# One transformer trunk layer on one core: the last down-projection group with its first transposes between the halves of its last product, embedding quarters around them, and the first two gate tiles in halves

## The chip, the cores and the metric

The kernel runs on one core of a Trainium2 chip. The metric is the device time of one execution in microseconds (us); lower is better. Times of a kernel are given as the median of several runs. A profile is of one execution; its span is the time from the first to the last instruction.

The engines are named as in the profile: PE is the tensor engine (matmuls; PEld is its weight loads), DVE the vector engine, ACT the scalar engine, POOL is GpSimd, and SP issues most DMAs.

## What is computed

The reference is one layer on 512 tokens of width 1024. A retention branch and a latent attention branch come first. Only the end of the layer matters here:

```
h2 = rms_norm(x, norm_mlp)
x = x + jnp.square(jax.nn.relu(h2 @ w_up)) @ w_down

gate = jax.nn.sigmoid(rms_norm(x, norm_ple) @ w_ple_gate)
x = x + gate * (p_l @ w_ple)
return x
```

`w_up` is 1024 x 4096, `w_down` 4096 x 1024, `w_ple_gate` 1024 x 1024, `p_l` 512 x 256 and `w_ple` 256 x 1024.

## The kernel before, in words

Every operand of a matmul is split into a high part and a low part (`split`, L289, and for weights `load_chunk`, L243: ACT writes the high part, L254, DVE the rest, L255), and each product is three matmuls: high by low, low by high, high by high (`mm3`, L279). A group of 24 matmuls of 512 columns makes one tile of 128 x 512 out of a 1024-long sum.

Weights come as blocks of 128 x 1024 (512 KB) through two helpers. `prepare` (L214) issues the DMA, up to three keys ahead; `load_chunk` splits the block, one key ahead. The split blocks have three buffers, the raw ones three or, for the down projection, seven. Some down blocks are sums of weight blocks: `prepare` has GpSimd issue a DMA that adds onto the raw block in SBUF (L225). Product 6's block is product 7's with one more block added, and product 4's is product 6's with another.

The work is a list of steps, (key of the weight, function, arguments), which is walked in order by `run_steps` (L258). Each engine gets its instructions from that list; a scheduler sets the order in which different engines' work interleaves within an engine, but PE keeps the list's order. So the order of steps around the change is the order on PE.

**The down projection** runs in four groups of 1024 rows of `w_down`. Each group is made by seven block products instead of eight, numbered 1 to 7: `combine` (L852) makes sums of activation blocks and splits them, `down` (L881) does one half (`c` = 0 or 1, 12 matmuls) of a product in PSUM, and `down_out` (L892) adds the product to `d`, the sum over groups. `d` is two tiles; its four blocks are c11, c12, c21, c22, and products go to them by the table in `down_out`: c11 is complete after products 1 and 2, c21 after 1, 6 and 4 (and what has been summed in PSUM), c22 after 5, and c12 after 3. Products 6, 5 and 3 accumulate in the PSUM tile of product 1, and 4 in that of 7 (`onto`, L879). In the first three groups the `up` products of the next group stand between these (`"u"` in `seq`, L1103). In the last group, which has none to prepare, `"u"` stands for a quarter of `p_l @ w_ple` (`ple`, L913, 12 matmuls and one ACT copy); in the trace its tile is `pw`.

**The end.** `reload_x2` (L923) reads x before the MLP back from DRAM into two tiles; `turn(n)` (L929, n = 0 to 3) transposes two column blocks of `d` by 8 instructions on PE (`tr`), adds them to x (L936), splits the result with the gain into `x3g` k = 2n and 2n + 1 (L937), and squares it for the norm (L941, summed in L945). `turn` 0 and 1 read c11 and c21; `turn` 2 and 3 read c12 and c22. `ple_gate(n)` (L952) multiplies eight tiles `x3g` by one tile of the gate's weight, into `pg`; `token_stats` (`stx`, L821) and `token_factor` (`pbx` on PE, copied to `bcx` by ACT, L829) make the norm's factor for each token; `ple_out` (L962) scales, applies the sigmoid, multiplies, adds and stores one tile of 128 rows of the output. The eighth tile is done in two halves of 256 tokens.

PSUM of this tail is a pool `PP` (L814) of four tiles, each of two banks.

Of the kernel before, what the change touches and what calls it, by code (L numbers as in the profile page):

```python
# [36 lines left out]
P = 128  # L37
# [17 lines left out]
GROUPS = DFF // 1024  # L55
# [89 lines left out]
def trunk_layer(ctx: ExitStack, tc: tile.TileContext, xT, pT, pos, gains, const, decay, wstream, outT):  # L145
# [18 lines left out]
    def MM(*a, **k):  # L164
        return tc.keep_in_program_order(nc.tensor.matmul(*a, **k))  # L165
# [38 lines left out]
    def step(key, fn, *args):  # L204
        steps.append((key, fn, args))
# [73 lines left out]
    def mm3(ps, stat, mov, first, last, **k):  # L279

        (sh, sl), (mh, ml) = stat, mov
        MM(ps, sl, mh, start=first, stop=False, **k)
        MM(ps, sh, ml, start=False, stop=False, **k)
        MM(ps, sh, mh, start=False, stop=last, **k)

    def cut(pair, a, n=P):
        return pair[0][:, a:a + n], pair[1][:, a:a + n]
# [30 lines left out]
    def stats(st, sq, rows=P, mov=None, first=True, last=True):  # L318

        mov = ones[0:rows, 0:1] if mov is None else mov  # L320
        for b in range(4):
            MM(st[:, b], sq[0:rows, b * P:b * P + P], mov, start=first and b == 0, stop=last and b == 3,
               skip_group_check=True)

    def blocks(ps, c):
        return ps[:, 0:4 * c].rearrange("p (b c) -> p b c", c=c)
# [8 lines left out]
    V = {}  # L335
# [54 lines left out]
    def mean_rsqrt(name, st, n):  # L390

        a, r = sm(name + "a"), sm(name, keep=True)
        TS(a, st.rearrange("p b c -> p (b c)"), 1.0 / n, EPS, op0=ALU.mult, op1=ALU.add)
        rsqrt(r, a, 4)
        return r, a
# [393 lines left out]
    x2g, x3g = [], [None] * 8  # L789
# [17 lines left out]
    def open_tail():  # L807
        head.close()
        t = tail.enter_context
        tail_pool["a"] = t(tc.tile_pool(name="tacts", bufs=1, reuse_waits="tile"))  # L810
        tail_pool["w"] = t(tc.tile_pool(name="tw", bufs=NDRAW, reuse_waits="tile"))
        tail_pool["p"] = t(tc.tile_pool(name="tpsum", bufs=4, space=bass.MemoryType.PSUM, reuse_waits="tile"))

    def PP(name):  # L814

        return tail_pool["p"].tile([P, 2, S], F32, tag="pp", name=name)
# [2 lines left out]
        return tail_pool["a"].tile([P, *shape], dtype, tag=tag, name=name, bufs=bufs)  # L819

    def token_stats(name, key):  # L821
        st = blocks(PP("st" + name)[:, 0], 1)
        stats(st, V[key])
        V["r" + name], _ = mean_rsqrt("r" + name, st, D)

# [123 lines left out]

    pg_ps = {}  # L950

    def ple_gate(w, n, cuts=1):  # L952
        N = S // cuts
        ps = PP(f"pg{n}")
        pg_ps[n] = []
        for c in range(cuts):
            out = ps[:, c, 0:N]
            for k in range(8):
                mm3(out, cut(w, k * P), cut(x3g[k], c * N, N), k == 0, k == 7)
            pg_ps[n].append(out)  # L960

    def ple_out(n):  # L962
        N = S // len(pg_ps[n])
# [52 lines left out]
    for h in range(MH):  # L1016
        p, more = h // 2, h + 2 < MH
# [69 lines left out]
    for n in range(8):  # L1087
        step(("o", n), out_proj, n)
    step(None, open_tail)

    def up_pair(gg, pair):
        for n in (2 * pair, 2 * pair + 1):
            step(("up", gg, n), up, gg, n)
            if (gg, n) == (0, 0):
                step(None, token_stats, "x2", "sq2")
            elif (gg, n) == (0, 1):
                step(None, token_factor, "x2")
        step(None, up_out, gg, pair)
# [4 lines left out]
    seq = [1, "u", 7, "u", 6, 2, "u", 5, 4, "u", 3]  # L1103
    order = [p for p in seq if p != "u"]
    step(None, combine, 0, 1)
    for gg in range(GROUPS):
        u = 0
        for p in seq if gg + 1 < GROUPS else [1, 7, "u", "u", 6, 2, 5, "u", 4, "u", 3]:
            if p == "u":
                if gg + 1 < GROUPS:  # L1110
                    up_pair(gg + 1, u)
                else:
                    if u == 0:
                        step(None, ple_in)
                    step(("ple", u // 2), ple, u)
                u += 1
                continue
            i = order.index(p)
            if p != 3:
                step(None, combine, gg, order[i + 1])  # L1120
            elif gg + 1 < GROUPS:
                step(None, combine, gg + 1, 1)
            if gg == GROUPS - 1 and p == 4:
                step(None, reload_x2)
            for c in range(2):
                step(("dp", gg, p, c), down, gg, p, c)
            step(None, down_out, gg, p)
    for n in range(4):
        step(None, turn, n)
    step(("pg", 0), ple_gate, 0)  # L1130
    step(None, token_stats, "x3", "sq3")
    step(("pg", 1), ple_gate, 1)
    step(None, token_factor, "x3")
    step(None, ple_out, 0)
    step(None, ple_out, 1)
    for n in range(2, 8):
        step(("pg", n), ple_gate, n, 2 if n == 7 else 1)
        step(None, ple_out, n)
    run_steps()

# [42 lines left out]
```

## Time and profile before

| | |
|---|---|
| median of 3 runs | 1153.18 us (1152.47 to 1153.44) |
| the profiled execution | 1154.78 us |
| its span, first to last instruction | 1153.0 us |
| mean granted PE clock | 0.998 of full speed |
| PE busy | 1125.0 us (98% of the span) |
| DVE busy | 699.9 us (61%) |
| ACT busy | 484.3 us (42%) |
| HBM traffic | 126.25 MB read, 4.19 MB written |

A row of the timeline has the start in us from the span's start, the duration, the engine, the source line, the operation and its operands as output<-inputs; instructions alike that follow each other are merged, with their count behind an x. In brackets stands how long the engine was idle before, and whose end released it. The chain of waits has start, duration and what ran. A row of the windows has the stretch, its length, busy time and count of PE, PEld, DVE, ACT and POOL, then the granted PE clock, the busy share of the DMA engines, and GB/s. PE's matmuls are pipelined: a row's duration overlaps the next row, so the pace is read from the starts.

### The profile page before, as it was taken

Reading aid. Unit: us, or ns where it says so; the run is one execution under the profiler, and the core shown is the slowest. Engines: PE = TensorE matmul, PEld = TensorE weight load, DVE = VectorE, ACT = ScalarE, POOL = GpSimd, SP = SyncE. Lnnn points to the kernel's source line nnn. Section 1 sums busy time; section 2 is a strip of 40 time slices with the busy share of each in tenths; the row PEclk is TensorE's granted clock in tenths of the full one; section 3 lists DMA queues with packets and bytes.
Section 4 is the critical chain, followed back from the end, with each engine's and each line's share of the span. In section 5 each row is a group of like instructions: output and inputs, shape, how many; then the busy total and the mean of one; then the engine's idle time right before and its main releaser. Section 6 shows DMA issues by size and latency. Waiting matters only on the chain.

```text
span 1153.0 us, 13664 instructions
## 1 busy us (share of the span) xinstructions
PE 1125.0 (98%) x5300; PEld 936.6 (81%) x5300; DVE 699.9 (61%) x1138; ACT 484.3 (42%) x682; POOL 29.1 (3%) x38
## 2 busy tenths in 40 slices
PE   7998999999999999999999999999999999999988
PEld 5877878888888888888888888788888888887766
DVE  5777586653447257545735766555466657667674
ACT  6446556442234243233324333434444434445531
POOL 0000000000000000000000000000001001001000
PEclk9999999999999999999999999999999999999999
DMA  6223131133212322321332234685567567567221
GB/s 202 69 71 108 47 87 47 55 124 107 92 55 92 121 74 69 107 92 55 110 103 73 74 97 147 185 300 138 137 188 173 150 180 170 162 173 175 92 73 55
DMA packets 43344, 133.42 MB, mean 116 GB/s; under 512 B 5296, under 2 KB 6576, under 8 KB 43024
## 3 DMA queue, kind: packets, MB, share of 16 engines
q1 hardware_dynamic: 38400, 115.36, 29.8%
q0 software_dynamic: 4736, 17.18, 8.5%
q8 instruction: 41, 0.67, 0.2%
q14 instruction: 23, 0.19, 0.0%
q10 hardware_dynamic: 144, 0.03, 0.0%
HBM read 126.25 MB, written 4.19 MB: 113 GB/s over the span
## 4 chain that ended last, share of the span: by engine, by line
PE 90%; DVE 5%; DMA 2%; ACT 1%; issue 1%; SPq 0%; DVEq 0%; ACTq 0%
PE up L165 15%; PE dn L165 11%; PE rg L165 8%; PE br L165 8%; PE rv L165 8%; PE rq L165 4%; PE rk L165 4%; PE gr L165 4%; PE bm L165 4%; PE pg L165 4%; PE gm L165 3%; PE ro L165 3%; PE wo L165 2%; PE sc L165 2%; PE pA L165 1%; PE pcq L165 1%
## 5 line engine op out<-in xcount | busy, mean ns | idle before, releaser
L254 ACT ACTIVATE wh_dp<-dr 128x1024 fp32r<-128x1024 f32 x56 | 59.2, 1061 | 121.0 <-PE up L165 83.6
L255 DVE TENSOR_TENSOR wl_dp<-dr,wh_dp 128x1024 fp32r<-128x1024 f32 x56 | 68.3, 1222 | 55.2 <-ACT wh_dp L254 55.2
L165 PE MATMUL dn<-wl_dp,ch 128*128 128x512 f32 x224 | 87.3, 390 | 0.7 <-DVE wl_dp L255 0.7
L165 PE MATMUL dn<-wh_dp,cl 128*128 128x512 f32 x224 | 87.2, 389 | 0.0
L165 PE MATMUL dn<-wh_dp,ch 128*128 128x512 f32 x224 | 87.2, 389 | 0.0
L254 ACT ACTIVATE wh_up<-wr_up 128x1024 fp32r<-128x1024 f32 x32 | 33.9, 1060 | 59.0 <-PE up L165 29.3
L225 POOL DMA_DIRECT2D dr<-wstream x32 | 27.6, 872 | 1029.0 <-DMA dr<-wstream 858.7
L165 PEld LDWEIGHTS dn<-wl_dp,ch 128*128 128x128 f32 x224 | 42.0, 188 | 9.9 <-DVE wl_dp L255 1.3
L255 DVE TENSOR_TENSOR wl_up<-wr_up,wh_up 128x1024 fp32r<-128x1024 f32 x32 | 39.1, 1223 | 17.7 <-ACT wh_up L254 17.6
L165 PEld LDWEIGHTS dn<-wh_dp,cl 128*128 128x128 f32 x224 | 42.0, 188 | 8.9
L165 PEld LDWEIGHTS dn<-wh_dp,ch 128*128 128x128 f32 x224 | 42.0, 188 | 8.6
L844 DVE SCALAR_TENSOR_TENSOR f<-up,bcx 128x512 f32<-128x512 f32 x32 | 20.6, 686 | 44.3 <-PE up L165 44.3
L255 DVE TENSOR_TENSOR wl_rg<-wr_rg,wh_rg 128x1024 fp32r<-128x1024 f32 x16 | 19.6, 1226 | 36.7 <-ACT wh_rg L254 36.7
L254 ACT ACTIVATE wh_rv<-wr_rv 128x1024 fp32r<-128x1024 f32 x16 | 17.0, 1060 | 55.3 <-PE br L165 26.2
L255 DVE TENSOR_TENSOR wl_rv<-wr_rv,wh_rv 128x1024 fp32r<-128x1024 f32 x16 | 19.6, 1226 | 32.8 <-ACT wh_rv L254 32.8
L254 ACT ACTIVATE wh_rg<-wr_rg 128x1024 fp32r<-128x1024 f32 x16 | 17.0, 1062 | 46.2 <-PE rv L165 35.0
L746 DVE TENSOR_TENSOR z<-rg,rbc 128x512 f32<-128x512 f32 x16 | 11.1, 692 | 39.7 <-PE rg L165 39.7
L254 ACT ACTIVATE wh_br<-wr_br 128x1024 fp32r<-128x1024 f32 x16 | 17.0, 1062 | 41.7 <-issue 18.8
L902 DVE TENSOR_TENSOR d<-d,dn 128x1024 f32<-128x1024 f32 x24 | 29.3, 1219 | 5.7 <-PE dn L165 5.7
L765 DVE TENSOR_TENSOR ret<-ret,br 128x512 f32<-128x512 f32 x24 | 16.5, 687 | 18.2 <-PE br L165 18.1
L622 ACT ACTIVATE p<-p,ng,hr 128x128 f32<-128x128 f32 (+3 forms) x32 | 20.7, 647 | 15.1 <-DVE ng L620 15.1
L255 DVE TENSOR_TENSOR wl_br<-wr_br,wh_br 128x1024 fp32r<-128x1024 f32 x16 | 19.5, 1220 | 3.5 <-ACT wh_br L254 3.5
(1590 smaller groups left out, 3383.5 us busy)
## 6 DMA issues: line engine op xcount, KB each, us to landing
dr<-wstream SPq DMA_DIRECT2D x40, 512.0 KB, 4.4
wr_up<-wstream SPq DMA_DIRECT2D x32, 512.0 KB, 4.3
dr<-wstream POOLq DMA_DIRECT2D x32, 512.0 KB, 5.8
wr_rv<-wstream SPq DMA_DIRECT2D x16, 512.0 KB, 3.4
wr_rg<-wstream SPq DMA_DIRECT2D x16, 512.0 KB, 3.5
wr_br<-wstream SPq DMA_DIRECT2D x16, 512.0 KB, 3.5
wr_gm<-wstream SPq DMA_DIRECT2D x16, 256.0 KB, 2.6
wr_bm<-wstream SPq DMA_DIRECT2D x8, 512.0 KB, 3.4
```

Of the source, the lines that this page charges most:

```text
L165: return tc.keep_in_program_order(nc.tensor.matmul(*a, **k))
L225: nc.gpsimd.dma_start(raw, chunk(("d", gg, kb, fb, c)), accum_op=ALU.add)
L254: ACT(hi, raw, AF.Copy)
L255: TT(lo, raw, hi.bitcast(F32), op=ALU.subtract)
L622: ACT(cols[b], cols[b], AF.Exp, bias=ng[:, b:b + 1], scale=d["rq"][:, b], accum_out=sums[:, b:b + 1])
L746: TT(z, ps, V["rbc"], op=ALU.mult)
L765: TT(ret[n], ret[n], ps, op=ALU.add)
L844: STT(u[:, i], ps[:, i], 0.0, V["bcx2"], op0=ALU.max, op1=ALU.mult)
L902: TT(to, to, dps[p], op=ALU.add if sign > 0 else ALU.subtract)
```

## The change

In the last group the order of products becomes 1, 7, 2, 6, 5, 4, 3. Two quarters of the embedding product stand after 2 and after 6; the other two move behind product 3. `turn(0)` and `turn(1)` stand between the two halves of product 3; `turn(2)` and `turn(3)` behind the last quarter. The reload of x2 is called at product 6 instead of 4. `ple_gate` can do half of the sum: tiles 0 and 1 first do k = 0 to 3 both, then k = 4 to 7 both. The third gate tile comes before the broadcast of the norm's factor, where the second did. The two halves of the eighth gate tile get a PSUM tile each. The PSUM tile for the statistics of x2 is taken when the tail's pools open.

```
     def ple_gate(w, n, part=None, cuts=1):
         N = S // cuts
         if n not in pg_ps:
             pg_ps[n] = [PP(f"pg{n}{c}")[:, 0, 0:N] for c in range(cuts)]
         for c, ps in enumerate(pg_ps[n]):
             for k in range(8) if part is None else range(4 * part, 4 * part + 4):
                 mm3(ps, cut(w, k * P), cut(x3g[k], c * N, N), k == 0, k == 7)
```

```
-        for p in seq if gg + 1 < GROUPS else [1, 7, "u", "u", 6, 2, 5, "u", 4, "u", 3]:
+        for p in seq if gg + 1 < GROUPS else [1, 7, 2, "u", 6, "u", 5, 4, 3]:
...
+            if gg == GROUPS - 1:
+                order = [1, 7, 2, 6, 5, 4, 3]
...
-            if gg == GROUPS - 1 and p == 4:
+            if gg == GROUPS - 1 and p == 6:
                 step(None, reload_x2)
             for c in range(2):
                 step(("dp", gg, p, c), down, gg, p, c)
+                if gg == GROUPS - 1 and p == 3 and c == 0:
+                    step(None, turn, 0)
+                    step(None, turn, 1)
             step(None, down_out, gg, p)
-    for n in range(4):
-        step(None, turn, n)
-    step(("pg", 0), ple_gate, 0)
+    step(("ple", 1), ple, 2)
+    step(("ple", 1), ple, 3)
+    step(None, turn, 2)
+    step(None, turn, 3)
+    for part in range(2):
+        for n in range(2):
+            step(("pg", n), ple_gate, n, part)
     step(None, token_stats, "x3", "sq3")
-    step(("pg", 1), ple_gate, 1)
+    step(("pg", 2), ple_gate, 2)
     step(None, token_factor, "x3")
     step(None, ple_out, 0)
     step(None, ple_out, 1)
-    for n in range(2, 8):
-        step(("pg", n), ple_gate, n, 2 if n == 7 else 1)
+    step(None, ple_out, 2)
+    for n in range(3, 8):
+        step(("pg", n), ple_gate, n, None, 2 if n == 7 else 1)
         step(None, ple_out, n)
```

What it moves on the engines is shown at three places, with the numbers that the built program gives its tiles. The first is PE at the border between the two halves of product 3 of the last group (`dn31` is the PSUM tile of products 1, 6, 5 and 3; `dp_3_3_0` and `dp_3_3_1` are the two halves' weights). Before:

```order
L165 MATMUL dn31_8316<-wh_dp_3_3_0_8604,cl33_8579 128x512
L165 MATMUL dn31_8316<-wl_dp_3_3_0_8605,ch33_8578 128x512
L165 MATMUL dn31_8316<-wh_dp_3_3_0_8604,ch33_8578 128x512
L165 MATMUL dn31_8316<-wh_dp_3_3_1_8637,cl33_8579 128x512
L165 MATMUL dn31_8316<-wl_dp_3_3_1_8638,ch33_8578 128x512
L165 MATMUL dn31_8316<-wh_dp_3_3_1_8637,ch33_8578 128x512
```

After:

```order
L165 MATMUL dn31_8316<-wl_dp_3_3_0_8584,ch33_8561 128x512
L165 MATMUL dn31_8316<-wh_dp_3_3_0_8583,ch33_8561 128x512
L165 MATMUL tr0_8620<-cst_80,d0_6682 128x128 x2
L165 MATMUL tr0_8620<-cst_80,d1_6683 128x128 x2
L165 MATMUL tr0_8620<-cst_80,d0_6682 128x128 x2
L165 MATMUL tr0_8620<-cst_80,d1_6683 128x128 x2
L165 MATMUL tr1_8640<-cst_80,d0_6682 128x128 x2
L165 MATMUL tr1_8640<-cst_80,d1_6683 128x128 x2
L165 MATMUL tr1_8640<-cst_80,d0_6682 128x128 x2
L165 MATMUL tr1_8640<-cst_80,d1_6683 128x128 x2
L165 MATMUL dn31_8316<-wh_dp_3_3_1_8602,cl33_8562 128x512
L165 MATMUL dn31_8316<-wl_dp_3_3_1_8603,ch33_8561 128x512
```

Sixteen transposes, those of column blocks 0 to 3, moved in front of the second half.

The second is DVE from product 4's addition to `d` on (`d1` += `dn37`; `dn31` is then product 3's, `x30` and `x31` are the reloaded x, `wl_pg` the low part of a gate tile's weight, `wl_ple` that of the embedding's). Before:

```order
L902 TENSOR_TENSOR d1_6683<-d1_6683,dn37_8358 128x2x512
L255 TENSOR_TENSOR wl_dp_3_3_1_8638<-dr_33111_8590,wh_dp_3_3_1_8637 128x1024
L255 TENSOR_TENSOR wl_pg_0_8656<-wr_pg_0_8608,wh_pg_0_8655 128x1024
L255 TENSOR_TENSOR wl_pg_1_8760<-wr_pg_1_8641,wh_pg_1_8759 128x1024
L902 TENSOR_TENSOR d0_6682<-d0_6682,dn31_8316 128x2x512
L936 TENSOR_TENSOR x30_8582<-x30_8582,tr0_8674 128x1024
L936 TENSOR_TENSOR x30_8582<-x30_8582,tr1_8694 128x1024
L298 SCALAR_TENSOR_TENSOR x3g0l_8685<-x30_8582,gn_81,x3g0h_8684 128x512
L936 TENSOR_TENSOR x31_8584<-x31_8584,tr2_8715 128x1024
L298 SCALAR_TENSOR_TENSOR x3g1l_8689<-x30_8582,gn_81,x3g1h_8688 128x512
```

After:

```order
L903 TENSOR_TENSOR d1_6683<-d1_6683,dn37_8358 128x2x512
L255 TENSOR_TENSOR wl_ple_1_8662<-wr_ple_1_8587,wh_ple_1_8661 128x1024
L937 TENSOR_TENSOR x30_8465<-x30_8465,tr0_8620 128x1024
L937 TENSOR_TENSOR x30_8465<-x30_8465,tr1_8640 128x1024
L298 SCALAR_TENSOR_TENSOR x3g0l_8631<-x30_8465,gn_81,x3g0h_8630 128x512
L255 TENSOR_TENSOR wl_pg_0_8681<-wr_pg_0_8606,wh_pg_0_8680 128x1024
L298 SCALAR_TENSOR_TENSOR x3g1l_8635<-x30_8465,gn_81,x3g1h_8634 128x512
L946 TENSOR_TENSOR sq30_8638<-sq30_8638,sq31_8658 128x1024
L298 SCALAR_TENSOR_TENSOR x3g2l_8651<-x30_8465,gn_81,x3g2h_8650 128x512
L903 TENSOR_TENSOR d0_6682<-d0_6682,dn31_8316 128x2x512
L298 SCALAR_TENSOR_TENSOR x3g3l_8655<-x30_8465,gn_81,x3g3h_8654 128x512
L255 TENSOR_TENSOR wl_pg_1_8760<-wr_pg_1_8665,wh_pg_1_8759 128x1024
```

The additions of the first two transposes and their four splits moved ahead of the addition of product 3, and the two gate weights' splits moved among them. Behind these rows follow `x31` += `tr2`, `x31` += `tr3`, and the rest up to `x3g7l`, with the split of gate tile 2's weight among them.

The third is PE at the broadcast of the norm's factor (`pbx3`), with what each row waits for in brackets. Before:

```order
L165 MATMUL pg1_8816<-x3g7h_8750,wh_pg_1_8759 128x512
L165 MATMUL pbx3_8841<-cst_80,rx3_8796 128x128 [waits DVE_49,PE_49]
L165 MATMUL pbx3_8841<-cst_80,rx3_8796 128x128 x3
L165 MATMUL pg2_8866<-x3g0h_8684,wl_pg_2_8811 128x512 [waits PE_49]
L165 MATMUL pg2_8866<-x3g0l_8685,wh_pg_2_8810 128x512
```

After:

```order
L165 MATMUL pg20_8847<-x3g7h_8750,wh_pg_2_8778 128x512
L165 MATMUL pbx3_8872<-cst_80,rx3_8827 128x128 [waits DVE_49,PE_49]
L165 MATMUL pbx3_8872<-cst_80,rx3_8827 128x128 x3
L165 MATMUL pg30_8903<-x3g0h_8630,wl_pg_3_8842 128x512 [waits Activation_49]
L165 MATMUL pg30_8903<-x3g0l_8631,wh_pg_3_8841 128x512
```

The tile behind the broadcast is now the fourth gate tile, and its first matmul waits for ACT; in the built program that is ACT's copy of the broadcast, and `pbx3` and `pg30` lie in the same two PSUM banks (`pbx3` and `pg2` did not).

More of the change, by code (lines that the diff above doesn't have):

```diff
@@ L812, in open_tail @@
         tail_pool["p"] = t(tc.tile_pool(name="tpsum", bufs=4, space=bass.MemoryType.PSUM, reuse_waits="tile"))
+        V["stx2"] = PP("stx2")
     def PP(name):
@@ L821, in token_stats @@
     def token_stats(name, key):
-        st = blocks(PP("st" + name)[:, 0], 1)
+        st = blocks((V["stx2"] if name == "x2" else PP("st" + name))[:, 0], 1)
         stats(st, V[key])
@@ L950, in trunk_layer @@
     pg_ps = {}
-    def ple_gate(w, n, cuts=1):
+    def ple_gate(w, n, part=None, cuts=1):
         N = S // cuts
[L954 to L960, printed above, removed]
+        if n not in pg_ps:
+            pg_ps[n] = [PP(f"pg{n}{c}")[:, 0, 0:N] for c in range(cuts)]
+        for c, ps in enumerate(pg_ps[n]):
+            for k in range(8) if part is None else range(4 * part, 4 * part + 4):
+                mm3(ps, cut(w, k * P), cut(x3g[k], c * N, N), k == 0, k == 7)
     def ple_out(n):
```

## The prediction

> **What bounds the kernel now.** I read the page first, then the chain that ended last over the final 93 us, then the tensor engine's (PE's) timeline where that chain leaves it, then the clock by windows. The page's first line says where the time is:
>
> ```profile
> PE 1125.0 (98%) x5300; PEld 936.6 (81%) x5300; DVE 699.9 (61%) x1138; ACT 484.3 (42%) x682; POOL 29.1 (3%) x38
> ```
>
> PE has work nearly all the time, so an edit that leaves its work alone can only win what PE waits, or loses to a slower clock. The chain of waits, with columns start, duration and what ran, shows where that is:
>
> ```profile
> 1061.75 10.95 PE dn L165 x47
> 1072.69 2.72 PE pw L165 x12
> 1075.41 5.44 PE dn L165 x24
> ...
> 1090.19 2.35 DVE x L936 x2
> 1092.54 0.66 DVE x3g0l L298
> 1093.20 1.13 DVE x L936
> ...
> 1098.59 1.14 DVE sq L945
> ...
> 1106.82 7.19 PE pg L165 x24
> 1114.01 0.44 PE pbx L165 x4
> 1114.44 32.99 PE pg L165 x168
> ```
>
> Up to 1089 and after 1106 the chain lies on PE; between them it lies on the vector engine (DVE), which turns the last sum `d` into the gate product's input. A matmul of the 512-wide kind costs 5.44/24 = 0.227 us in the row at 1075.41; the 24 at 1106.82 take 7.19. PE's timeline has the waits themselves (in brackets: idle before, and who ended it):
>
> ```profile
> 1049.67 0.39 PE L165 MATMUL pw<-pph,wl_ple 128*128 128x512 f32 x1
> ...
> 1061.75 0.50 PE L165 MATMUL dn<-wl_dp,ch 128*128 128x512 f32 x1 [0.70 <-DVE wl_dp L255]
> ...
> 1072.53 0.39 PE L165 MATMUL pw<-pph,wl_ple 128*128 128x512 f32 x1
> ...
> 1088.86 3.65 PE L165 MATMUL tr<-cst,d 128*128 128x128 f32 x32
> 1092.27 0.48 PE L165 MATMUL pg<-x3g0h,wl_pg 128*128 128x512 f32 x1
> 1093.26 0.50 PE L165 MATMUL pg<-x3g0l,wh_pg 128*128 128x512 f32 x1 [0.51 <-DVE x3g0l L298]
> ...
> 1105.87 0.94 PE L165 MATMUL stx<-ones,sq 128*128 128x1 f32 x8
> 1106.68 0.64 PE L165 MATMUL pg<-x3g0h,wl_pg 128*128 128x512 f32 x1
> ```
>
> **What is there to win.** Three losses, each a stretch of PE less its work.
> (a) From the first embedding matmul `pw` at 1049.67 to the next pair's at 1072.53 are 22.86 us, for 24 `pw` and 72 `dn`, 96 x 0.2267 = 21.76. Lost 1.10, most of it at 1061.75, where DVE's split of a weight block came late.
> (b) From the first transpose at 1088.86 to 1106.68 are 17.82 us, for 32 transposes (3.41 to the first `pg`), 24 matmuls (5.44) and the sums `stx` (0.81). Lost 8.16.
> (c) The next 24 matmuls take 7.17 us (1106.68 to the broadcast `pbx` at 1113.85, quoted below) instead of 5.44. Lost 1.73, to the clock: the column behind the engines' is the granted clock,
>
> ```profile
> 1080.00:1100.00 20.00, 16.65 (x85) 12.79 (x83) 16.24 (x17) 12.14 (x15) 0.00 (x0) 1.00 0.16 54
> 1106.00:1108.00 2.00, 2.00 (x13) 1.71 (x12) 0.98 (x7) 1.06 (x1) 0.00 (x0) 0.71 0.00 0
> 1108.00:1110.00 2.00, 2.00 (x6) 1.61 (x5) 1.86 (x7) 0.00 (x0) 0.00 (x0) 0.50 0.00 0
> ```
>
> half speed just after a dozen microseconds in which PE mostly waited. Together 10.99 us.
>
> **Part by part.** *Product order and embedding quarters.* PE's rows are the same as before to the end of product 7, at 1049.67 (the first `pw` row). Without waits PE then runs, at 2.72 us per half product or quarter: product 2 to 1055.11, quarter 0 to 1057.83, 6 to 1063.27, quarter 1 to 1065.99, 5 to 1071.43, 4 to 1076.87, first half of 3 to 1079.59, 16 transposes to 1081.29, second half to 1084.01, quarters 2 and 3 to 1089.45, 16 transposes to 1091.15. The question is whether everything arrives. Products 6 and 4 read a weight block onto which GpSimd's DMA adds; the issues, and ACT's first use of what they left:
>
> ```profile
> 1044.37 0.86 POOL L225 DMA_DIRECT2D dr<-wstream  x1 [0.83 <-DVE wl_dp L255]
> 1054.49 0.86 POOL L225 DMA_DIRECT2D dr<-wstream  x1 [9.26 <-DVE wl_dp L255]
> ...
> 1055.66 1.06 ACT L254 ACTIVATE wh_dp<-dr 128x1024 fp32r<-128x1024 f32 x1 [2.71 <-DMA dr<-wstream]
> ...
> DMA to landing us min/median/max: 3.4/5.4/11.2
> ```
>
> Product 6's second half landed at 1055.66, 11.2 us after its issue. It is now wanted at 1060.55 instead of 1057.83; with 1.06 on ACT and 1.22 on DVE (a 1024-wide instruction, worked out below) behind the landing, it has 2.5 us of room. The queue that the moved steps pass is SP's, where these stood:
>
> ```profile
> 1047.51 0.33 SPq L240 DMA_DIRECT2D wr_pg<-wstream  x1
> 1061.72 0.33 SPq L221 DMA_DIRECT2D dr<-wstream  x1
> ...
> 1070.06 0.43 SPq L926 DMA_DIRECT2D x<-x2d  x1
> ...
> x<-x2d SPq DMA_DIRECT2D x1, 1024.0 KB, 5.8
> ```
>
> The last block of product 3 (1061.72) now goes out when product 2's block is split, about 1047, in the place of the gate tile's load of equal size; that load and the 1 MB reload of half of x2 follow about 1052.5. So the traffic that meets product 6's block is the same till its last 3 us. Product 4's additions are issued as before (about 1055 and 1058) and wanted, with the 2.3 us of their splits, at 1069 and 1072; 11.2 us still make it. GpSimd's own order is unchanged. The other splits, 1.06 and 1.22 each and one per 2.72 us of matmuls, come out 1 us or more ahead of their halves. I take nothing for a wait here, with 2 us as the bound, and the whole of (a) as won.
>
> *First transposes between the halves.* They need column blocks c11 and c21 of `d`, whose last addition follows product 4: 1076.87, 0.2 till a matmul's end is seen (a row of 0.39 us stands in a slot of 0.23), and 1.22 (two such in the row at 1090.19 take 2.35, of which the chain counts 1.13 till the next begins): 1078.3, before PE is through the first half at 1079.59. 2.72 us of matmuls cover it; without them it would cost 1.4.
> Then DVE is the question. From the first addition of x (`tr0` ends at 1080.44, DVE starts 0.2 later) to `x3g7l`, the last input of the gate product, it has by its order eleven 1024-wide instructions and eight 512-wide ones: at the chain's 1.14 and 0.66, and 0.1 for the last one's end, 17.9, plus 0.4 in which it waits for the third transposes: done at 1098.95. PE, not waiting, has 12 + 12 gate matmuls with k below 4 (to 1096.59) and reaches `x3g7l` at 1098.86, ten matmuls into the next part. **The two chains meet within 0.2 us.** What hid nothing before now hides nearly all: 2.72 + 5.44 + 5.44 us of product 3, quarters and gate tile 1 stand beside DVE's work. I charge 0.17 of waiting; ahead is PE's bound, so this can only fall to 0, and each microsecond that DVE is late costs one. Of (b) and (c), then, all but 0.17 is won: PE is never half idle for long, so I take the clock to stay at 1.00.
>
> *The new wait.* In the new program the broadcast `pbx` and gate tile 3 have the same pair of PSUM banks, as three tiles now live at once; tile 3 must wait till ACT has copied the broadcast. Before, the same copy stood behind a weight split on ACT and nobody waited for it:
>
> ```profile
> 1113.85 0.60 PE L165 MATMUL pbx<-cst,rx 128*128 128x128 f32 x4
> 1114.05 1.06 ACT L254 ACTIVATE wh_pg<-wr_pg 128x1024 fp32r<-128x1024 f32 x1 [6.92 <-PE pg L165]
> 1114.20 0.48 PE L165 MATMUL pg<-x3g0h,wl_pg 128*128 128x512 f32 x1
> 1115.01 0.58 ACT L829 ACTIVATE bcx<-pbx 128x512 f32<-128x512 f32 x1
> ```
>
> The split waits for the last matmul ahead of the broadcast and is now tile 5's, with the same relation. So PE, which went on at 1114.20, goes on at 1115.59: 1.39 us lost. Queued behind are gate tiles 3 to 7, so all of it shows. Nothing would be lost if the slots differed; I see no way to more than 1.6.
>
> *The last tile.* Its halves were two slices of one PSUM tile, now two tiles:
>
> ```profile
> 1147.46 0.76 DVE L967 TENSOR_TENSOR zg<-pg,bcx 128x256 f32<-128x256 f32 x2 [2.94 <-PE pg L165]
> 1147.92 0.75 ACT L968 ACTIVATE zg<-zg 128x256 f32<-128x256 f32 x2 [4.85 <-DVE zg L967]
> 1148.37 0.76 DVE L969 TENSOR_TENSOR zg<-zg,pw 128x256 f32<-128x256 f32 x2 [0.15 <-ACT zg L968]
> 1149.05 0.75 DVE L970 TENSOR_TENSOR zg<-zg,x 128x256 f32<-128x256 f32 x2
> 1149.49 0.81 SPq L971 DMA_DIRECT2D outT<-zg  x2
> ```
>
> The first half waited for the second. Now it can leave during the second's 2.7 us of matmuls, and one half runs after PE: multiply at 1147.46, sigmoid 1147.92, multiply 1148.37, add 1148.83 (one 0.42 later), store 1149.27, where the second store left at about 1149.92. 0.65 won; between 0 and 0.8.
>
> *The PSUM tile of the x2 statistics* is taken earlier; its slot and that of the first `up` tile stay the same: nothing.
>
> **The sum.** 10.99 + 0.65 - 0.17 - 1.39 = 10.08. The span of 1153.0 becomes 1142.9, the profiled execution's 1154.78 becomes 1144.7; the runs' median of 1153.18, 1.6 below that execution, becomes **1143.1 us**.
>
> [...] The row: 32 transposes in a run, 1088.86 to 1092.27, lie in the window 1080 to 1100, whose granted clock is 1.00. [...]
>
> **Rivals.** *DVE late.* The two chains are so close that a delay anywhere among 19 instructions shows, with waits `[.. <-DVE x3g..]` at k 4 to 7 and, if long, a piece of (c). At 0.5 to 3 us, typically 1.5: 1144.6. For: in that stretch DVE waits in turn for ACT's high parts and PE's transposes, and the row at 1093.26 shows PE waiting for just these outputs. Chance 0.20.
> *Weights late.* Product 6's block lands 1 to 3 us after its room, as the 1 MB reload shares the DMA engines: 1145.1. Against: 2.5 us of room. 0.07.
> *Clock.* A half-speed stretch like that of (c) appears behind the transposes: 1.73 each, for two 3.46: 1146.6. 0.05.
> *No overlap.* The first transposes release nothing, say since the reload of x2 comes late; then (b) and (c) come back and only (a) and the last tile are won, less the new wait: 1152.8. Against: the reload is issued some 27 us before its use. 0.03.
> *Slower.* Product 4's added block, issued behind the reload, is so late that PE stands. It costs from a landing at 1069 on, one for one; beyond the kernel before by over 0.2% (2.3 us) it needs 10.1 + 2.3 = 12.4 us, a landing at 1081.4, 26 us after the issue, where the longest row above is 11.2: 1155.5. 0.02.
>
> **How the numbers follow.** The forecast has 0.63. Its own range is 1141.7 (no new wait) to 1144. With DVE late and weights late it reaches to 1146.2, and 1141.5 below takes in the bound of the last tile: that holds over 8 in 10, the clock's single stretch included. About 0.2%, 2.3 us, can be told from no change here: faster 0.95 (all but the last two), same 0.03, slower 0.02.
>
> **What would show it.** Right: PE without a gap over 0.3 us from 1050 to the first `pg` matmul at about 1091; `stx` near 1102; a gap of 1.4 ended by ACT `bcx` ahead of tile 3 (near 1109); clock 1.00 in every window from 1080; one half chain behind PE. Wrong: a `dn` matmul that waits for `wl_dp`, gaps ended by `x3g` with k above 3, clock below 1.00, or a tile 3 that doesn't wait.

## The result and the profile after

The changed kernel takes 1145.17 us (median of 4 runs, 1144.17 to 1146.36); the kernel before took 1153.31 beside it (4 runs, 1152.47 to 1155.58). The ratio is 0.9927, with a 95% interval of 0.9910 to 0.9944: 8.1 us faster, where 10.1 were forecast (1143.1). The profiled execution took 1144.94 us with a span of 1143.2; the forecast for it was 1144.7 and 1142.9. In the runs further below, one of e5's ten executions, the profiled one, took 2298.57 us; it is left out of e5's median and ratio, and e11 is the profile of that kernel.

PE's row on the page shows that the work stayed and the waiting went: 5300 matmuls as before, busy time 4.9 us less (1125.0 before), in a span that is 9.8 us shorter.

```profile
PE 1120.1 (98%) x5300; PEld 935.0 (82%) x5300; DVE 700.0 (61%) x1138; ACT 484.9 (42%) x682; POOL 29.1 (3%) x38
```

The chain of waits of the changed kernel, over the stretch that the prediction worked through:

```profile
1065.99 13.60 PE dn L165 x60
1079.59 1.75 PE tr L165 x16
1081.34 2.75 PE dn L165 x12
1084.09 5.44 PE pw L165 x24
1089.53 1.75 PE tr L165 x16
1091.28 11.14 PE pg L165 x48
1102.42 0.79 PE stx L165 x8
1103.21 5.62 PE pg L165 x24
...
1108.85 1.06 ACT wh_pg L254
1109.91 0.49 ACT bcx L830
...
1110.44 27.86 PE pg L165 x144
...
1138.33 0.44 DVE zg L967
...
1138.79 0.42 ACT zg L968
...
1139.23 0.43 DVE zg L969
...
1139.69 0.42 DVE zg L970
```

Where the chain of before left PE for 16 us (1089.0 to 1105.3), nearly all of them on DVE, this one stays on PE from 1066 to 1109. It leaves PE for the copy of the broadcast, which stands behind a weight split on ACT, and again for one half tile at the end. The last 24 matmuls ahead of the broadcast take 5.62 where they took 7.19. The windows (columns as before, the granted clock behind the engines') show full speed, and PE without a pause until the new wait:

```profile
1080.00:1090.00 10.00, 10.00 (x55) 8.52 (x54) 9.50 (x10) 7.44 (x10) 0.00 (x0) 1.00 0.31 107
1090.00:1100.00 10.00, 10.00 (x51) 8.20 (x50) 9.10 (x11) 6.40 (x9) 0.00 (x0) 1.00 0.30 105
1100.00:1105.00 5.00, 5.00 (x27) 4.26 (x26) 2.81 (x8) 1.84 (x2) 0.00 (x0) 1.00 0.30 104
1105.00:1110.00 5.00, 4.25 (x21) 3.30 (x19) 1.49 (x8) 1.15 (x2) 0.00 (x0) 1.00 0.32 106
```

PE's timeline has one row with a wait from 1085 to the end:

```profile
1110.44 0.50 PE L165 MATMUL pg<-x3g0h,wl_pg 128*128 128x512 f32 x1 [1.19 <-ACT bcx L830]
```

DVE's timeline shows why PE no longer waits for it. Its chain now starts at 1080.50 and is through at 1098.89, beside product 3, the quarters and half the gate tiles; the addition of product 3 to `d` stands in the middle:

```profile
1080.50 2.35 DVE L937 TENSOR_TENSOR x<-x,tr 128x1024 f32<-128x1024 f32 x2 [1.24 <-PE tr L165]
...
1087.03 1.22 DVE L903 TENSOR_TENSOR d<-d,dn 128x1024 f32<-128x1024 f32 x1
...
1090.44 2.35 DVE L937 TENSOR_TENSOR x<-x,tr 128x1024 f32<-128x1024 f32 x2 [0.40 <-PE tr L165]
...
1098.15 0.74 DVE L298 SCALAR_TENSOR_TENSOR x3g7l<-x,gn,x3g7h 128x512 fp32r<-128x512 f32 x1
```

### The profile page after: what moved, and what is told of

It is laid out like the page before. It is cut to its first block, busy times and chain, and to the rows that moved or that the text cites. A ratio compares the mean times of both kernels' runs of the same rounds, so it can differ in the third digit from the quotient of the medians.

```text
span 1143.2 us, 13662 instructions
## 1 busy us (share of the span) xinstructions
PE 1120.1 (98%) x5300; PEld 935.0 (82%) x5300; DVE 700.0 (61%) x1138; ACT 484.9 (42%) x682; POOL 29.1 (3%) x38
## 3 DMA queue, kind: packets, MB, share of 16 engines
HBM read 126.25 MB, written 4.19 MB: 114 GB/s over the span
## 4 chain that ended last, share of the span: by engine, by line
PE 93%; DVE 3%; DMA 2%; ACT 1%; issue 0%; SPq 0%; ACTq 0%; DVEq 0%
PE up L165 15%; PE dn L165 13%; PE rg L165 8%; PE br L165 8%; PE rv L165 8%; PE pg L165 4%; PE rq L165 4%; PE rk L165 4%; PE gr L165 4%; PE bm L165 4%; PE gm L165 3%; PE ro L165 3%; PE wo L165 2%; PE sc L165 2%; PE pcq L165 1%; PE rs L165 1%
## 5 line engine op out<-in xcount | busy, mean ns | idle before, releaser
L254 ACT ACTIVATE wh_rv<-wr_rv 128x1024 fp32r<-128x1024 f32 x16 | 17.0, 1060 | 55.3 <-PE br L165 26.2
```

What stands on the lines that cost most here:

```text
L254: ACT(hi, raw, AF.Copy)
```

## Experiments

The theory was the prediction's sum. The gain is PE's waits for DVE (b), together with a late weight block (a) and the half clock (c), less a new wait of 1.4 us. The first rival was that one part does the work alone: the new order, the halves of the gate tiles or the last tile. The second was that the place of the transposes decides, by far more than the tie of 0.17. A third question came up with the first runs: why the medians moved by 8 to 9 us when the two profiles differ by 10.

Executions of one kernel reach the first `up` matmul at different times (747.5 to 750.6 in the 13 profiles here), long before the change. So the profiles are compared by the time from that matmul to the end of the span, called the *stretch*. For before it is 1153.0 - 748.9 = 404.1 us, and for after 1143.2 - 748.75 = 394.4. A median has those up to 3.1 us in it, so a difference of a microsecond or two between medians of six runs is read with care.

| kernel | median us (runs) | ratio to before [95%] | span - first `up` = stretch |
|---|---|---|---|
| e1 after, unchanged | 1144.47 (6) | 0.9923 [0.9908, 0.9938] | 1144.1 - 749.7 = 394.4 |
| e2 turns behind product 3 | 1146.81 (6) | 0.9936 [0.9921, 0.9952] | 1145.3 - 750.5 = 394.8 |
| e3 gate tiles whole | 1148.72 (6) | 0.9956 [0.9939, 0.9972] | 1146.8 - 749.7 = 397.1 |
| e4 broadcast in its own banks | 1143.51 (6) | 0.9916 [0.9899, 0.9933] | 1141.3 - 748.4 = 392.9 |
| e5 quarters and order as before | 1151.58 (9) | 0.9984 [0.9972, 0.9995] | (e11) |
| e6 before + new order | 1153.07 (10) | 0.9990 [0.9976, 1.0005] | 1151.5 - 747.7 = 403.8 |
| e7 before + gate halves | 1151.54 (10) | 0.9982 [0.9970, 0.9994] | 1150.6 - 750.4 = 400.2 |
| e8 before + last tile | 1153.23 (10) | 1.0002 [0.9990, 1.0014] | 1151.7 - 749.9 = 401.8 |
| e9 before, one run | 1153.14 (1) | | 1151.3 - 750.0 = 401.3 |
| e10 before, one run | 1156.02 (1) | | 1154.2 - 750.6 = 403.6 |
| e11 as e5, one run | 1150.58 (1) | | 1148.8 - 747.5 = 401.3 |
| e12 as e6, one run | 1151.41 (1) | | 1149.6 - 748.5 = 401.1 |

Beside e1 to e4 the kernel before took 1153.58 (11 runs), beside e5 to e8 1153.45 (31 runs); the one run beside e9 to e12 took 1155.75.

**e1: the changed kernel again.** No edit.

> The changed kernel once more, unchanged, with more rounds: how much of the 9.8 us between the two profiled spans (1153.0 and 1143.2) stands in the median. By the sum of the prediction, 10.1 us less than the kernel before in the runs too, ratio 0.991 to 0.992. Rival: a part of the gain is in one of the two profiled executions only, and the medians differ by about 8 us, ratio 0.993.

It gained 9.1 us between the medians (1153.58 - 1144.47), halfway between the 10.1 and the 8 of the rival, and its stretch is that of after. The changed kernel's end repeats; which of the two holds is a question of before, and e9 and e10 look at it.

**e2: the first two turns behind product 3.**

```
-                if gg == GROUPS - 1 and p == 3 and c == 0:
-                    step(None, turn, 0)
-                    step(None, turn, 1)
             step(None, down_out, gg, p)
+    step(None, turn, 0)
+    step(None, turn, 1)
     step(("ple", 1), ple, 2)
```

> The changed kernel with the first two turns behind product 3 instead of between its halves, all else kept. PE's sum of work is the same. Theory of the tie: DVE's additions of the product 3 block and two weight splits move ahead of its long chain, 15.6 us of it are left behind the first transposes instead of 17.9, so x3g7l comes only 0.2 to 0.5 us later than in the changed kernel, and the time is that of the changed kernel plus 0.2 to 0.5. Rival, the cover counted as a whole: half a product less (2.72 us) beside DVE's chain, plus 2.5 us, as gaps before the k 4 to 7 matmuls.

The stretch is only 0.4 longer, and PE's one further wait in e2's timeline is at the meeting point of the two chains. DVE's timeline of e2 shows why it is so little:

```profile
1101.06 0.50 PE L165 MATMUL pg<-x3g7l,wh_pg 128*128 128x512 f32 x1 [0.30 <-DVE x3g7l L298]
```

```profile
1082.48 1.23 DVE L255 TENSOR_TENSOR wl_pg<-wr_pg,wh_pg 128x1024 fp32r<-128x1024 f32 x1 [1.45 <-ACT wh_pg L254]
1084.11 1.22 DVE L903 TENSOR_TENSOR d<-d,dn 128x1024 f32<-128x1024 f32 x1 [0.40 <-PE dn L165]
1085.24 2.35 DVE L937 TENSOR_TENSOR x<-x,tr 128x1024 f32<-128x1024 f32 x2
```

Counted from the first `up`, DVE starts on x 3.0 us later (1085.24 - 750.51 against 1080.50 - 748.75). But a weight's split and the addition of product 3, 1.13 each to the next start, are then done ahead of the chain, and the 0.40 that DVE waited inside it falls away: 2.66 of the 3.0 come back. In the profile the place between the halves is worth 0.4, and the 2.5 us of gaps that the rival has there are not there. The medians are 2.3 apart (1146.81 - 1144.47). The profiled e2 reached its first `up` 0.8 later than the profiled e1 and 1.8 later than after, ahead of all that the edit moves; the other five runs have no profile, so most of the 2.3 stays unexplained.

**e3: gate tiles 0 and 1 whole.**

```
-    for part in range(2):
-        for n in range(2):
-            step(("pg", n), ple_gate, n, part)
+    for n in range(2):
+        step(("pg", n), ple_gate, n)
```

> The changed kernel with gate tiles 0 and 1 each done whole, 0 first. Theory: DVE's chain ends as in the changed kernel (x3g7l near 1098.9), but PE has 12 matmuls less to do before it needs it, so it waits 2.7 us more in k 4 to 7, and the time is the changed kernel's plus 2.7, with the clock at 1.00. Rival: the waits let the clock fall as in the kernel before, plus 4.4. Other rival: PE was the bound and the halves buy nothing, plus 0 to 0.3.

The stretch is 2.7 longer, as expected, and the granted clock is 1.00 from 1060 to 1140. The medians are 4.3 apart, which is nearer to the rival's 4.4; whether the half clock came in runs without a profile is not shown. PE's timeline has the waits that the halves hide:

```profile
1096.27 0.50 PE L165 MATMUL pg<-x3g5l,wh_pg 128*128 128x512 f32 x1 [0.43 <-DVE x3g5l L298]
1098.07 0.50 PE L165 MATMUL pg<-x3g6l,wh_pg 128*128 128x512 f32 x1 [0.84 <-DVE x3g6l L298]
1099.86 0.50 PE L165 MATMUL pg<-x3g7l,wh_pg 128*128 128x512 f32 x1 [0.83 <-DVE x3g7l L298]
```

**e4: tiles 0 and 1 in the two banks of one PSUM tile,** so that the broadcast and gate tile 3 no longer share theirs.

```
+            if n == 0:
+                V["pg01"] = PP("pg01")
-            pg_ps[n] = [PP(f"pg{n}{c}")[:, 0, 0:N] for c in range(cuts)]
+            pg_ps[n] = [V["pg01"][:, n, 0:N]] if n < 2 else [PP(f"pg{n}{c}")[:, 0, 0:N] for c in range(cuts)]
```

> The changed kernel with gate tiles 0 and 1 in the two banks of one PSUM tile, so that the broadcast of the norm's factor and gate tile 3 have slots of their own. Theory: the wait of 1.4 us ahead of tile 3 goes and nothing takes its place: the changed kernel's time less 1.4. Rival: the output chain of tiles 0 to 2 behind the copied factor then holds tile 4's slot, and less than half of it is won.

Its 1143.51 us are the lowest median of all the kernels, though the interval of its ratio overlaps with e1's. The chain of e4 no longer leaves PE at the broadcast, and the stretch is 1.5 shorter:

```profile
1102.86 5.61 PE pg L165 x24
1108.47 0.44 PE pbx L165 x4
1108.90 27.55 PE pg L165 x144
```

**e5 and e11: the changed kernel with the order of products and the quarters of before.** The reload of x2 stays at product 6.

```
-        for p in seq if gg + 1 < GROUPS else [1, 7, 2, "u", 6, "u", 5, 4, 3]:
+        for p in seq if gg + 1 < GROUPS else [1, 7, "u", "u", 6, 2, 5, "u", 4, "u", 3]:
...
-            if gg == GROUPS - 1:
-                order = [1, 7, 2, 6, 5, 4, 3]
...
-    step(("ple", 1), ple, 2)
-    step(("ple", 1), ple, 3)
```

> The changed kernel with the old product order and the old places of the four embedding quarters; the first turns still stand between the halves of product 3, and the first two gate tiles are still in halves. Theory: the loss (a) of 1.1 us is back, and without 5.44 us of quarters beside it PE reaches the end of the first gate tiles some 4 us before DVE's chain ends: the changed kernel's time plus 5 (4 to 6), clock at 1.00. Rival: the halves alone hide the chain, and only (a) comes back, plus 1.1.

> The changed kernel with the old product order and the old places of the quarters, for its profile. Theory: PE waits about 4 to 5 us in the second halves of the first two gate tiles, and from the first up matmul to the end are 399 to 400.5 us (changed kernel: 394.4). Rival: only the stall of 1.1 us amid the products comes back, 395.5.

Most of the gain is gone: 1.9 us are left of it in the medians, and e11's stretch is 6.9 longer than after's. Its timeline and windows have the place. The first transposes come early, but behind product 3 PE has nothing to do until DVE, in the middle of its chain, has added product 3:

```profile
1060.20 0.50 PE L165 MATMUL dn<-wl_dp,ch 128*128 128x512 f32 x1 [0.60 <-DVE wl_dp L255]
...
1093.55 2.74 PE L165 MATMUL tr<-cst,d 128*128 128x128 f32 x16 [4.30 <-DVE d L903]
```

```profile
1094.00:1096.00 2.00, 2.00 (x15) 2.00 (x13) 2.00 (x3) 0.00 (x0) 0.00 (x0) 0.63 0.03 8
1096.00:1098.00 2.00, 2.00 (x7) 1.61 (x6) 2.00 (x3) 1.64 (x3) 0.00 (x0) 0.52 0.79 248
```

PE waits 4.30 us and then runs at half clock; ahead of that (a) is back, with 0.95. It is more than was expected: in e11's chain 16 transposes took 2.74 and the 48 gate matmuls 11.74, where after's took 1.75 and 11.14, 1.6 us for the clock. The three make 6.85 of the 6.9. So the two quarters (5.44 us) behind the early transposes are what fills the wait. Product order and quarters were only moved together; what each does alone is not shown.

**e6 and e12: before with the new order and quarters alone.** The four turns stay together, behind the last quarter.

```
-        for p in seq if gg + 1 < GROUPS else [1, 7, "u", "u", 6, 2, 5, "u", 4, "u", 3]:
+        for p in seq if gg + 1 < GROUPS else [1, 7, 2, "u", 6, "u", 5, 4, 3]:
...
+            if gg == GROUPS - 1:
+                order = [1, 7, 2, 6, 5, 4, 3]
...
-            if gg == GROUPS - 1 and p == 4:
+            if gg == GROUPS - 1 and p == 6:
...
+    step(("ple", 1), ple, 2)
+    step(("ple", 1), ple, 3)
     for n in range(4):
         step(None, turn, n)
```

> The kernel before with only the new product order and the new places of the quarters (two of them between product 3 and the transposes); all turns behind them, gate tiles whole. Theory: (a) is won, 1.1 us, and the addition of product 3's block, 1.1 us on DVE, is hidden by the quarters: the kernel before less 2.2; the waits at k 0 to 7 and the half clock stay. Rival: the quarters' place is worth the whole cover, less 5.4.

> The kernel before with only the new product order and the new places of the quarters, for a second profile. Theory: the stall amid the products (1.1) and the addition of product 3 on DVE (1.1) are gone; 402.4 - 2.2 = 200.2 + 200 = 400.2 us from the first up matmul to the end where the half clock lies inside the waits, up to 402 where it lies behind them. Rival: no gain beyond the 1.1, 401.3 or more with the half clock inside.

No difference that can be told (0.9990, interval over 1). e12 has neither (a) nor a half clock ahead of its last matmul (1.00 from 740 to 1130, and the 168 `pg` matmuls behind the broadcast took 32.99, as in before) and is the clean one. Its stretch is 0.2 below that of e9, which has neither either. I had expected about 1.1 from hiding the addition of product 3. The addition (on DVE at 1082.12) is hidden, but DVE then waits for the transposes:

```profile
1088.43 2.35 DVE L936 TENSOR_TENSOR x<-x,tr 128x1024 f32<-128x1024 f32 x2 [3.96 <-PE tr L165]
```

It starts 1.07 behind the first transpose (1087.36); in before that was 1090.19 - 1088.86 = 1.33. Only the difference is won. That expectation fell.

**e7: before with the gate tiles in halves alone** (and tile 2 ahead of the broadcast, as in the change; the last tile's halves stay in one PSUM tile).

```
...
-    step(("pg", 0), ple_gate, 0)
+    for part in range(2):
+        for n in range(2):
+            step(("pg", n), ple_gate, n, part)
     step(None, token_stats, "x3", "sq3")
-    step(("pg", 1), ple_gate, 1)
+    step(("pg", 2), ple_gate, 2)
...
```

> The kernel before with only the first two gate tiles in halves (and so the third tile ahead of the broadcast). Theory: 12 of tile 1's matmuls fill PE's waits, less 2.7 us; PE is then busy enough that the half clock of 3.4 us does not come, less 1.7 more; the new wait ahead of tile 3 costs 1.4: the kernel before less 3.0. Rival, the clock falls all the same: the kernel before less 1.3.

It won 1.9 us in the medians, between the 3.0 of the theory and the 1.3 of the rival. Against e9 the stretch is 1.1 shorter: 2.7 from the halves (e3), less the new wait, which stands here too (1.20 us, ended by ACT `bcx`). The profile has no half clock between the first `up` and the last matmul (1.00 from 740 to 1140, and the last 144 matmuls took 27.86, as in after), but neither has e9's, so it does not show that the halves keep it away.

**e8: before with only the last tile's halves in PSUM tiles of their own.**

```
-        ps = PP(f"pg{n}")
...
-            out = ps[:, c, 0:N]
+            out = PP(f"pg{n}{c}")[:, 0, 0:N]
```

> The kernel before with only the two halves of the eighth gate tile in a PSUM tile each. Theory: one half chain instead of two behind the last matmul, 0.65 us less (0.5 to 0.8), read from the profile as the time from the last matmul to the last store's issue. Rival: the two halves' chains did not add up, nothing.

The chain at e8's end has one half behind PE, as after's has:

```profile
1146.87 0.43 DVE zg L966
...
1148.24 0.42 DVE zg L969
```

The store leaves at 1148.69, 1.82 behind the multiply; in before the last one left at about 1149.92, 2.46 behind the multiply at 1147.46. So 0.64 is won in the profile; the medians, with an interval of 0.1% to both sides, don't show it.

**e9 and e10: the kernel before again, twice.** No edit.

> The kernel before, unchanged, one more profiled execution. Theory: PE's waits of 13 us before x3g7l always bring a stretch of half clock of 3.4 us, but its place moves from execution to execution; where it lies inside the waits it costs nothing, where it lies behind them 1.7 us. From the first up matmul to the end of the span: 402.4 us if it lies inside, 404.1 if behind, between these if it straddles. Rival: the half clock always follows the waits, 404.1 each time.

> The kernel before, unchanged, another profiled execution, as the one ahead: 402.4 to 404.1 us from the first up matmul to the end by the place of the half clock. Rival: 404.1 each time.

These two answer the question of the medians. The 24 matmuls ahead of the broadcast, in the chain of e9:

```profile
1106.78 5.56 PE pg L165 x24
```

and in e10, with the stall (a) ahead:

```profile
1061.71 1.24 DVE wl_dp L255
...
1062.99 10.96 PE dn L165 x47
...
1108.06 7.17 PE pg L165 x24
```

e9 has neither (a), as its 72 `dn` matmuls run in one piece, nor (c). e10 has both, 2.3 us longer: 0.6 for (a), counted as the prediction counts it, and 1.6 for (c). The theory that PE's waits bring a half clock in every execution of this kernel fell.

## Why the prediction was right, and where its size was off

**(a), the late block.** Right: in after, PE's timeline marks no wait from 1050 to 1109. The chain of before tells where the stall comes from: ACT waited for the block that is added onto product 6's, 11.18 us on its way, and so came late to the split of the next block, product 2's, for which PE waited:

```profile
1044.37 11.18 DMA dr<-wstream
...
1055.66 0.13 ACT wh_dp L254
...
1059.49 0.96 ACT wh_dp L254
...
1060.47 1.24 DVE wl_dp L255
...
1061.75 10.95 PE dn L165 x47
```

In the new order product 2 stands ahead of 6. The stall stood in the chain or timeline of four of the six profiled executions with the old order (before, e8, e10, e11, not e7 and e9), where it cost 0.6 to 1.15 us, and in none of the seven with the new one.

**(b), PE's waits for DVE.** Right. `x3g7l` was done at 1098.89 (forecast 1098.95), and the tie cost 0.1 (0.17 charged; the prediction's own two times are 0.09 apart). `stx` stands at 1102.42 in the chain (about 1102). It was the combination that won it. From e9's 401.3 the order alone takes 0.2, the halves alone 1.1 (with the new wait in it) and the last tile about 0.65; all together take 6.9. The parts need each other: DVE's chain of 18 us starts early because of the early transposes, and PE has work to do beside it because of the quarters and the halves. The prediction's aside that without cover the first transposes would cost 1.4 was not tried: e2, too, has matmuls ahead of them.

**(c), the clock.** Right for after: 1.00 in all its windows from 1070 to 1140. That a PE that is half idle for long brings the half clock was an estimate from one profile: e9 has the waits of before, and 1.00 behind them.

**The new wait.** Right: the start after the broadcast comes 1110.44 - 1108.65 = 1.79 behind it, where it was 0.35; lost 1.44 (forecast 1.39). e4 took it away and won 1.5.

**The last tile.** Right: from the multiply at 1138.33 to the store's issue at 1140.14 are 1.81 us in after and 1.82 in e8, where before had 2.46: 0.65.

**The sum.** For the profiled pair it held: 9.8 of span, forecast 10.1. The step that was off is the last one: *"the runs' median of 1153.18, 1.6 below that execution, becomes 1143.1 us"*. It took (a) and (c), 2.83 us together, from the median in full, though they were read from one execution that had both and stood above the median. Such executions are only a part: (a) stood in four of the six profiles with the old order, and of the seven with the late DVE chain of before (before, e6 to e10, e12) before, e6 and e10 lost about 1.5 us to the clock in the 24 matmuls (7.19, 7.06 and 7.17 where e7, e8, e9 and e12 took 5.56 to 5.62); e6, with a longer half clock, lost 2.7 in all against e12. Without both, the sum is 8.16 + 0.65 - 0.17 - 1.39 = 7.25; with shares of 4/6 of 1.10 and 3/7 of 1.73 it is, as an estimate, 7.25 + 0.73 + 0.74 = 8.7. Measured were 8.1 and 9.1.

The runs without a profile have only a mean granted clock: at 0.999, e1's four runs (1143.88 to 1144.75, median 1144.14) and four of the 31 of before (1150.73 to 1152.11, median 1151.59) are 7.45 us apart. That is close to the 7.25 but proves little: the mean says nothing of (a), and it counts a half clock wherever it lies; e9, without (c), has 0.998.

The measured 1145.2 lies above the forecast's own range (1141.7 to 1144) and inside the wide one (to 1146.2), which had its room for a late DVE and late weights; neither came, so that it held is in part luck.

**The rivals.** *DVE late* came no further than 0.1. *Weights late* didn't come: no `dn` matmul of after waits. The *clock* rival's stretch behind the transposes didn't come: 16 of them begin at 1079.59 and 16 at 1089.53, 1.75 us each time, and the windows behind have 1.00. *Slower* and *no overlap* are excluded by the timeline.

## What to carry to other kernels

Look for the work that can stand beside a chain on another engine, and move both ends: the early start and the halves without the quarters behind them won 1.9 us (e5), no more than the halves alone (e7); moving the work without starting early won nothing that could be told (e6), and all together won 8 to 9. Before a loss in a trace is subtracted from a median, ask whether every execution has it; the two further profiles of the kernel before (e9, e10) show (a) and (c) once both absent and once both there. And when tiles are made to live longer, see who shares their PSUM banks: here it cost 1.4 us that a paired tile gave back.

## What was not expected of the hardware

Five profiles (before, e6, e8, e10, e11) have a half clock between the transposes and the last matmul; in four of them it lasted 3.4 us, and it does not come in each execution. Windows of 1 us inside it have 0.50, so its length is twice the sum of (1 - clock) x length: in before, with 0.92, 0.50, 0.50, 0.50 and 0.87 from 1106 to 1111, 2 x 1.71 = 3.4 us; in e11 above, 2 x (0.37 x 2 + 0.48 x 2) = 3.4. In e10:

```profile
1108.00:1110.00 2.00, 2.00 (x7) 1.57 (x7) 1.73 (x7) 0.37 (x1) 0.00 (x0) 0.56 0.00 0
1110.00:1112.00 2.00, 2.00 (x7) 1.58 (x6) 1.29 (x7) 0.00 (x0) 0.00 (x0) 0.59 0.22 49
```

it is 2 x (0.88 + 0.82) = 3.4, and in e8:

```profile
1098.00:1102.00 4.00, 3.61 (x8) 1.90 (x9) 4.00 (x5) 2.69 (x5) 0.00 (x0) 0.58 0.00 0
```

2 x 0.42 x 4 = 3.4 again, there inside PE's waits, where it cost nothing that shows: the 24 matmuls took 5.61. In e6 the half clock lasted from 1094.9 to 1108.6, 13.7 us; in e12, the same kernel, there was none from the first `up` to the last matmul.

Behind the last matmul before and after have it too: 0.50 from 1152 to 1153 and from 1142 to 1143. Seven profiles (e1, e2, e3, e7 to e10) have a mean clock of 0.98 over the first 100 us, the other six 1.00. The seven reach the first `up` at 749.7 to 750.6 us, the six at 747.5 to 748.9, so a good part of the spread there goes with the slower clock.

What decides whether an execution has term (c) is not shown. PE's busy time ahead of it does not tell before and e9 apart: it was 4.05 and 4.06 us of the 7 from 1092 to 1099, and 4.20 and 4.19 of the 7 from 1099 to 1106; yet from 1106 to 1110 the clock was 0.61 in before and 1.00 in e9.
